# Sample index keys: gathers and their transposes issued apart, the transposes behind the products of the pair ahead

## The chip, the cores and the metric

The kernel runs on one core of a Trainium2 chip. The metric is the device time of one execution in microseconds; the figure given for a kernel is the median of several runs. A profiled execution gives the trace from which all rows below come.

## What is computed

The reference is one inference step of a decoder trunk of two layers (the constant in the reference, DEPTH = 2). A prompt of 1040 tokens (16 meta tokens and 1024 new ones) and a sample group of 8 sequences with 8 new tokens each share all weights. Each layer has three branches, a gated linear recurrence (HGRN2), a convolution module and a sparse attention, which are merged by gates and added to the residual stream. The change lies in the indexer of the sparse attention, which scores every key for every query; the 256 best keys are then attended to:

```python
def index_scores(qi, wi, ki):
    s = jnp.einsum('bqhd,bsd->bqhs', qi.astype(F32), ki.astype(F32))
    return jnp.einsum('bqhs,bqh->bqs', jax.nn.relu(s), wi.astype(F32) * IDX_SCALE)

def dsa_sample(...):
    ki_past = cache_kidx[page_table].reshape(nb, past, IDX_DIM)
    ki_all = jnp.concatenate([ki_past.astype(ki_new.dtype), ki_new], axis=1)
    sc = index_scores(qi, wi, ki_all)
    ...
```

For the sample group the index keys of the past (1024 keys of 64 numbers per sequence) lie in a paged cache and are fetched by the page table: eight sequences per layer, 256 KB each.

## The kernel before, in words

**The order of the work.** The kernel is written with a scheduling layer that gives every instruction its semaphores. TensorE runs in the order in which the program is written (the whole of it stands in a manual schedule for that engine), and so does VectorE from the start of a layer to the end of the mask stage. ScalarE, GpSimd and SyncE, which issues most transfers, are ordered by a planner from the program's order, its estimated durations and the times at which operands and buffers come free; once ordered, each of these queues is worked off strictly in turn.

**The filler.** A layer's dense projections are one stream of matmuls (L391, `stream`), cut into steps of three matmuls. Other stages call `fill(key)` to put so many steps between their own TensorE instructions, so that TensorE has work while they wait for other engines. A block of output needs 24 matmuls, 384 or 336 columns wide, into one of two `mm` tiles in PSUM; ScalarE evicts it (L204) to a tile `sp`. The weights of the stream come as 512 KB transfers on SyncE (L267), are rounded by ScalarE (`wh`, L269, the weight cast) and their remainder is formed on GpSimd (`wl`, L270, the weight split). In the same manner `taps(key)` puts steps of the depthwise convolution (L1503, L1504) into VectorE's order.

**The indexer.** It first prepares the prompt's keys, then scores six blocks of prompt queries with four heads each (the prompt's heads, `for i in range(7, 1, -1)`; behind each block GpSimd masks the diagonal, L814), and then comes to the sample. There the eight sequences are taken in four pairs, two groups of two pairs. For a sequence, GpSimd gathers 128 rows of eight keys by an indirect DMA (L887) into a tile `kir`, of which there are two. Four transposes on TensorE (L895) turn it into a PSUM tile `tp`, of which there are three. ScalarE copies its two halves (L899, L900) into the pair's tile `kib`, of which there is one. Two matmuls per sequence (L861, the products) multiply `kib` with the queries into the group's tile `lg`. So the next pair's copies cannot begin before this pair's products are done.

After two pairs the scores against the new keys follow (L865), then ScalarE's Relu, a matmul that adds up the heads (L835), and VectorE's additions into the score tile SC8 (L838 for the first group, L840 for the second and for the 16 meta queries, L876 and L877). Between transposes and products of a pair stand two `fill("ib")` of six steps each (36 matmuls) and two `taps("ts")`.

**Where the gathers and transposes stand.** `sample_kidx` issues the gather and the four transposes of one sequence and returns a function that makes the copies. It is called for pair 0 behind the prompt's heads and `fill("iw")`, and for pair i+1 right behind the copies of pair i: so the transposes of pair i+1 stand in TensorE's order ahead of the two `fill("ib")` and the products of pair i.

Of the kernel before, what the change touches and what calls it, by code (L numbers as in the profile page):

```python
# [154 lines left out]
def trunk(tc, a, o, depth=DEPTH):  # L155
# [35 lines left out]
    def lgt():  # L191
        return pair[0].tile([128, 1024], F32, name="lg", tag="lg")

    def tpt():
        return ptp.tile([128, 512], F32, name="tp", tag="tp")
# [7 lines left out]
    def act_(out, in_, fn, **kw):  # L203
        S.activation(out, in_, fn, **kw)  # L204
# [368 lines left out]
    def layer(l, hst, late):  # L573
# [46 lines left out]
        SC8 = scp.tile([128, NT], F32, name="SC8", tag="SC8")  # L620
        fill("ic")
        indexer(l, CTr, SC, SC8, fill, taps, act)
        ctr.close()
        tk1 = tks.enter_context(tc.tile_pool(name="tk1", bufs=1))
# [106 lines left out]
    def indexer(l, CTr, SC, SC8, fill, taps, act):  # L731
        with tc.tile_pool(name="ixc", bufs=1) as xc, tc.tile_pool(name="ixt", bufs=2) as xt:
# [28 lines left out]
            def qstack(t, rows):  # L761
                ps = tpt()
                for j in range(2):
                    T.transpose(ps[:, j * rows:(j + 1) * rows], CTr[0:rows, t, 256 + 128 * j:384 + 128 * j],
                                ident[0:rows, 0:rows])
                q = xt.tile([128, 2, 2, 128], F32R, name="qs", tag="qs")
                lo = ps[0:64, 0:2 * rows].rearrange("p (j n) -> p j n", j=2)
                hi = ps[64:128, 0:2 * rows].rearrange("p (j n) -> p j n", j=2)
                S.copy(q[0:64, :, 0, 0:rows], lo)
                S.copy(q[64:128, :, 1, 0:rows], hi)  # L770
                V.tensor_tensor(q[64:128, :, 0, 0:rows], lo, f(q[0:64, :, 0, 0:rows]), op=OP.subtract)
                V.tensor_tensor(q[0:64, :, 1, 0:rows], hi, f(q[64:128, :, 1, 0:rows]), op=OP.subtract)
                return q, lo, hi

            def qk(dst, q, h, rows, c0, c1):
                j, e = divmod(h, 2)
                T.matmul(dst, q[:, j, e, 0:rows], KIH[:, c0:c1], start=True, stop=False)
                T.matmul(dst, q[:, j, e, 0:rows], KIL[:, c0:c1], start=False, stop=True)
# [7 lines left out]
            for g in range(3):  # L786
# [4 lines left out]
                V.tensor_reduce(w1[0:m], w4[0:m], AX.X, OP.add)  # L791
                V.tensor_scalar(ws[0:m, g, :], cols[0:m, g, :], w1[0:m, 0:1], None, op0=OP.mult)
            fill("iq")
            for i in range(7, 1, -1):
                n = 128 * (i + 1)
                q = nxt[0]
                dst = SC[:, SCOFF[i]:SCOFF[i] + n]
                for h in range(4):
                    ps = lgt()
                    for c0 in range(0, n, 512):  # L800
                        c1 = min(n, c0 + 512)
                        qk(ps[:, c0:c1], q, h, 128, c0, c1)
                    if h == 1:
                        nxt = qstack(i - 1, 128) if i > 2 else qstack(8, 80)
                    fill("is", 7 - i)
                    rl = xt.tile([128, 1152], F32, name="rl", tag="rl")
                    act_(rl[:, 0:n], ps[:, 0:n], AF.Relu)
                    taps("ti", 7 - i)
                    if h == 0:
                        V.tensor_scalar(dst, rl[:, 0:n], wsc[:, i, 0:1], None, op0=OP.mult)  # L810
                    else:
                        V.scalar_tensor_tensor(dst, rl[:, 0:n], wsc[:, i, h:h + 1], dst, op0=OP.mult, op1=OP.add)  # L812
                dg = SC[:, SCOFF[i] + n - 128:SCOFF[i] + n]
                G.affine_select(dg, dg, pattern=[[-1, 128]], base=0, channel_multiplier=1, compare_op=OP.is_ge, fill=NEG)  # L814
# [10 lines left out]
            for h in range(4):  # L825
                j, e = divmod(h, 2)
# [4 lines left out]
            def gather(g, r):  # L831
                m = 128 if g < 2 else 64
                pg, pc = lgt(), pac.tile([128, 512], F32, name="ac", tag="ac")
                for (c0, c1), dst in zip(CH, (pg[0:80, 0:512], pg[0:80, 512:1024], pc[0:80, 0:80])):
                    T.matmul(dst, ws[0:m, g, :], r[0:m, c0:c1], start=True, stop=True)  # L835
                if g == 0:
                    S.copy(SC8[0:80, 0:1024], pg[0:80])
                    V.tensor_tensor(SC8[0:80, 1024:NT], pc[0:80, 0:80], cm80[0:80], op=OP.add)  # L838
                else:
                    V.tensor_tensor(SC8[0:80, 0:1024], SC8[0:80, 0:1024], pg[0:80], op=OP.add)  # L840
                    V.tensor_tensor(SC8[0:80, 1024:NT], SC8[0:80, 1024:NT], pc[0:80, 0:80], op=OP.add)

            fill("iw")

            kraw = [sample_kidx(l, e, xt) for e in range(2)]
            for g in range(2):
                ps = lgt()
                for b in (0, 2):
                    ki = xt.tile([128, 1024], F32, name="kib", tag="kib", bufs=1)
                    for e in range(2):  # L850
                        kraw[e](ki[64 * e:64 * e + 64])
                    taps("ts")
                    if 4 * g + b < 6:
                        kraw = [sample_kidx(l, 4 * g + b + 2 + e, xt) for e in range(2)]
                    fill("ib")
                    taps("ts")
                    fill("ib")
                    for n in range(2):
                        for e in range(2):
                            r, c0 = slice(64 * e, 64 * e + 64), 512 * (n ^ e)  # L860
                            T.matmul(ps[32 * (b + e):32 * (b + e) + 32, c0:c0 + 512],  # L861
                                     qs8[r, 4 * g + b + e].rearrange("p h q -> p (h q)"), ki[r, c0:c0 + 512],
                                     start=True, stop=True)
                px = tpt()
                T.matmul(px[:, 0:80], qs8[0:64, 4 * g:4 * g + 4].rearrange("p b h q -> p (b h q)"), ki8, start=True, stop=True)  # L865
                r = xt.tile([128, 1152], F32, name="rl", tag="rl")
                act_(r[:, 0:1024], ps, AF.Relu)
                act_(r[:, 1024:NT], px[:, 0:80], AF.Relu)
                fill("ir")
                gather(g, r)  # L870
                fill("ig")
# [6 lines left out]
            r = xt.tile([128, 1152], F32, name="rl", tag="rl")  # L878
# [5 lines left out]
    def gather_rows(dst, cache, l, bb):  # L884
        src = cache.rearrange("l n (g s) h d -> (l n g) (s h d)", s=8) if len(cache.shape) == 5 else \
            cache.rearrange("l n (g s) d -> (l n g) (s d)", s=8)
        G.indirect_dma_start(out=dst, out_offset=None, in_=src,  # L887
                             in_offset=bass.IndirectOffsetOnAxis(ap=rowid[:, l, bb:bb + 1], axis=0))

    def sample_kidx(l, bb, xt):  # L890
        raw = xt.tile([128, 8, 64], F32, name="kir", tag="kir")
        gather_rows(raw.rearrange("p s d -> p (s d)"), a["cache_kidx"], l, bb)
        ps = tpt()
        for j in range(4):
            T.transpose(ps[:, 128 * j:128 * j + 128], raw[:, 2 * j:2 * j + 2, :].rearrange("p j d -> p (j d)"), ident)  # L895

        def keys(ki):
            kv = ki.rearrange("p (n j e) -> p e j n", j=4, e=2)
            S.copy(kv[:, 0], ps[0:64].rearrange("p (j n) -> p j n", j=4))  # L899
            S.copy(kv[:, 1], ps[64:128].rearrange("p (j n) -> p j n", j=4))  # L900

        return keys
# [881 lines left out]
```

## Time and profile before

| | |
|---|---|
| median of 3 runs | 2891.84 us (2885.23 to 2892.67) |
| profiled execution, its own time | 2899.35 us |
| span of the profiled execution | 2897.4 us |
| instructions | 44994 |
| mean granted TensorE clock | 0.982 |

The profile counts for each engine the time in which an instruction of it ran. The timeline lists instructions in order of time; runs of equal instructions are merged (x8), and a bracket gives the time the engine had stood idle before and what ended it. PE is TensorE, DVE is VectorE, ACT is ScalarE, POOL is GpSimd. A granted clock of 1.00 is the full TensorE clock of 2.4 GHz, 0.50 is 1.2 GHz.

### The profile page before, as it was taken

To read this page: it belongs to the slowest core of one execution; us is meant where nothing else is said; L and a number is where in the kernel's file an instruction comes from. 1 tells how busy PE (TensorE), PEld (TensorE's weight loads), DVE (VectorE), ACT (ScalarE), POOL (GpSimd) and SP (SyncE) were. 2 spreads that over 40 slices of the span, in tenths; PEclk is the share of its full clock that TensorE was granted. 3 is DMA by queue.
4 is the path that set the end of the run, shared out by engine and by line. 5 is a ranking of instruction groups with operands and counts; after the bars stand their busy time and mean duration, and the time that the engine had idled before them with its cause. 6 is when DMAs were issued, how large, how long until landed. Compare 5 with 4: busy or idle time off the path is not lost. (4 is left out here: it accounts for less than half of the span.)

```text
span 2897.4 us, 44994 instructions
## 1 busy us (share of the span) xinstructions
PE 2751.2 (95%) x17094; PEld 2614.6 (90%) x17094; DVE 2120.3 (73%) x3832; ACT 1183.9 (41%) x2365; POOL 1249.3 (43%) x978
## 2 busy tenths in 40 slices
PE   7999899999998999989999998998999999999898
PEld 7999779999998898879999997898999989888798
DVE  5789887888969667445357798798899786774533
ACT  4324443332333556544341344422332345565432
POOL 3543344433434115756563342534444241158553
PEclk9999999999999999999999999999999999999999
DMA  4433233332244224656453233422331441256644
GB/s 153 152 93 101 91 122 124 115 124 94 98 157 152 76 68 154 213 190 190 149 170 95 88 102 101 166 77 103 119 130 62 158 151 57 87 162 219 198 156 150
DMA packets 192568, 374.14 MB, mean 129 GB/s; under 512 B 30656, under 2 KB 129696, under 8 KB 192288
## 3 DMA queue, kind: packets, MB, share of 16 engines
q1 hardware_dynamic: 166016, 272.21, 29.8%
q10 hardware_dynamic: 20448, 78.09, 6.7%
q0 software_dynamic: 5888, 20.97, 2.3%
q8 instruction: 134, 2.20, 0.3%
q14 instruction: 82, 0.67, 0.1%
HBM read 251.07 MB, written 122.40 MB: 129 GB/s over the span
## 5 line engine op out<-in xcount | busy, mean ns | idle before, releaser
L391 PE MATMUL mm<-xh,wh 128*128 128x384 f32 (+2 forms) x2656 | 887.9, 336 | 22.5 <-ACT sp L204 19.1
L391 PE MATMUL mm<-xl,wh 128*128 128x384 f32 (+2 forms) x2656 | 884.0, 335 | 0.0
L270 POOL TENSOR_TENSOR wl<-wr,wh 128x512 fp32r<-128x512 f32 x332 | 481.2, 1467 | 714.7 <-ACT wh L269 452.3
L391 PEld LDWEIGHTS mm<-xh,wh 128*128 128x128 f32 x2656 | 505.9, 190 | 36.8 <-ACT sp L204 24.5
L391 PE MATMUL mm<-xh,wl 128*128 128x384 f32 (+2 forms) x2656 | 530.4, 336 | 0.0
L391 PEld LDWEIGHTS mm<-xl,wh 128*128 128x128 f32 x2656 | 505.5, 190 | 7.1 <-issue 1.7
L391 PEld LDWEIGHTS mm<-xh,wl 128*128 128x128 f32 x2656 | 460.2, 191 | 6.2 <-issue 1.7
L923 DVE TENSOR_SCALAR_CACHE_REDUCE jk<-SC,F 80x1104 bf16<-80x1104 f32 (+6 forms) x448 | 448.8, 1002 | 8.4
L204 ACT ACTIVATE sp<-mm,vec 128x384 f32<-128x384 f32 (+1 forms) x356 | 198.6, 565 | 525.5 <-PE mm L391 509.9
L1503 DVE SCALAR_TENSOR_TENSOR cy<-up,vec,cy 128x1040 f32<-128x1040 f32 x240 | 333.1, 1388 | 0.4
L269 ACT CAST wh<-wr 128x512 fp32r<-128x512 f32 x352 | 203.5, 618 | 157.8 <-PE mm L391 76.6
L204 ACT ACTIVATE P<-P,nm 128x896 f32<-128x896 f32 (+7 forms) x128 | 99.5, 777 | 64.1 <-DVE nm L1028 62.2
L1044 DVE TENSOR_TENSOR pl<-tp,ph 128x512 fp32r<-128x512 f32 x144 | 97.7, 687 | 36.8 <-ACT ph L1043 36.1
L1504 DVE SCALAR_TENSOR_TENSOR cy<-us,vec,cy 128x64 f32<-128x64 f32 x240 | 118.3, 493 | 0.0
L1043 ACT CAST ph<-tp 128x512 fp32r<-128x512 f32 x144 | 83.2, 583 | 54.3 <-PE tp L1040 50.2
L1028 DVE CUSTOM_DVE_ANT_0 P<-sc,MB 128x512 f32<-128x512 f32 (+1 forms) x96 | 63.9, 667 | 56.5 <-PE sc L1022 55.7
L1353 PEld LDWEIGHTS lg<-hQ,hK 128*128 128x128 f32 x512 | 67.8, 210 | 28.0 <-issue 19.9
L1353 PE MATMUL lg<-hQ,hK 128*128 128x64 f32 x512 | 68.5, 292 | 25.5 <-DVE hQ L1382 25.4
L1032 DVE TENSOR_SCALAR P<-P,nm 128x896 f32<-128x896 f32 (+7 forms) x128 | 87.9, 687 | 4.3
L1040 PE MATMUL tp<-ident,P 128*128 128x128 f32 x576 | 87.5, 274 | 1.5 <-DVE P L1032 1.5
L204 ACT ACTIVATE rl<-lg 128x1024 f32<-128x1024 f32 (+6 forms) x54 | 42.6, 789 | 93.3 <-DVE SC L812 40.1
L287 PE MATMUL tp<-xh,wh 128*128 128x384 f32 (+2 forms) x240 | 79.0, 331 | 0.4 <-DVE z L1689 0.4
(454 smaller groups left out, 5914.7 us busy)
## 6 DMA issues: line engine op xcount, KB each, us to landing
wr<-in_wp SPq DMA_DIRECT2D x180, 512.0 KB
eg<-gateD SPq DMA_DIRECT2D x80, 184.0 KB
gateD<-sp ACTq DMA_DIRECT2D x24, 552.0 KB
gateD<-sp ACTq DMA_DIRECT2D x24, 544.0 KB
cr<-in_wc SPq DMA_DIRECT2D x16, 290.0 KB
gt<-gateD SPq DMA_DIRECT2D x24, 192.0 KB
za<-zaD SPq DMA_DIRECT2D x24, 192.0 KB
ggD<-sp ACTq DMA_DIRECT2D x8, 552.0 KB
```

Source lines behind the costliest of these rows:

```text
L204: S.activation(out, in_, fn, **kw)
L269: S.copy(wh[:, k:k + 4], wr[:, k:k + 4])
L270: (eng or G).tensor_tensor(wl[:, k:k + 4], wr[:, k:k + 4], f(wh[:, k:k + 4]), op=OP.subtract)
L391: T.matmul(ps, w, x, start=(j == 0), stop=(j == 23))
L923: V.tensor_scalar(jk[0:rows, 0:n], s, F.bitcast(F32)[0:rows, j:j + 1], None, op0=OP.is_ge, op1=OP.add, accum_out=cnt[0:rows, j:j + 1])
L1032: V.tensor_scalar(p[:, 0:n], p[:, 0:n], nm[:, 3:4], None, op0=OP.mult)
L1040: T.transpose(ps[:, 128 * c:128 * c + 128], P[c][:, 128 * kt:128 * kt + 128], ident)
L1043: S.copy(ph, ps)
L1044: V.tensor_tensor(pl, ps, f(ph), op=OP.subtract)
L1353: T.matmul(ps[:, 64 * c:64 * c + 64], K[:, 128 * c:128 * c + 128], up(Q[:, 128 * c:128 * c + 128], m), start=True, stop=True)
L1503: V.scalar_tensor_tensor(yp, up[:, j:j + 1040], w, yp, op0=OP.mult, op1=OP.add)
L1504: V.scalar_tensor_tensor(ys, us[:, :, j:j + 8], w, ys, op0=OP.mult, op1=OP.add)
```

## The change

`sample_kidx` is split in two: `kidx_rows` allocates `kir` and issues the gather; `kidx_turned` makes the four transposes and returns the copies. The gathers of pair 0 are issued ahead of the prompt's heads in the program's order, their transposes where they were. The gathers of pair i+1 stay where they were, right behind the copies of pair i; their transposes now come behind the products of pair i. Number and kind of all instructions, the buffers and the filler's steps are the same.

```diff
             fill("iq")
+
+            rows = [kidx_rows(l, e, xt) for e in range(2)]
             for i in range(7, 1, -1):
...
             fill("iw")
 
-            kraw = [sample_kidx(l, e, xt) for e in range(2)]
+            kraw = [kidx_turned(r) for r in rows]
             for g in range(2):
                 ps = lgt()
                 for b in (0, 2):
...
                     taps("ts")
                     if 4 * g + b < 6:
-                        kraw = [sample_kidx(l, 4 * g + b + 2 + e, xt) for e in range(2)]
+                        rows = [kidx_rows(l, 4 * g + b + 2 + e, xt) for e in range(2)]
                     fill("ib")
                     taps("ts")
                     fill("ib")
...
                                      start=True, stop=True)
+                    if 4 * g + b < 6:
+                        kraw = [kidx_turned(r) for r in rows]
                 px = tpt()
...
-    def sample_kidx(l, bb, xt):
+    def kidx_rows(l, bb, xt):
         raw = xt.tile([128, 8, 64], F32, name="kir", tag="kir")
         gather_rows(raw.rearrange("p s d -> p (s d)"), a["cache_kidx"], l, bb)
+        return raw
+
+    def kidx_turned(raw):
         ps = tpt()
         for j in range(4):
```

## Rows read from the trace of the kernel before

**Rows 1.** The page: busy us, share, instructions; and a group of evictions (mean ns).

```profile
PE 2751.2 (95%) x17094; PEld 2614.6 (90%) x17094; DVE 2120.3 (73%) x3832; ACT 1183.9 (41%) x2365; POOL 1249.3 (43%) x978
...
L204 ACT ACTIVATE sp<-mm,vec 128x384 f32<-128x384 f32 (+1 forms) x356 | 198.6, 565 | 525.5 <-PE mm L391 509.9
```

**Rows 2.** Waits of TensorE, whole run: us in total, times, longest.

```profile
PE tp L895 <- DMA kir<-in_cache_kidx,rowid: 7.8, 4, 3.4
...
PE tp L895 <- ACT kib L900: 4.6, 4, 1.7
...
PE lg L876 <- DVE SC L840: 1.4, 2, 0.8
```

**Rows 3.** Timeline of TensorE, layer 0, sample's pairs: start us, us, instruction, idle before.

```profile
316.99 1.03 PE L895 MATMUL tp<-ident,kir 128*128 128x128 f32 x8
...
321.27 0.63 PE L895 MATMUL tp<-ident,kir 128*128 128x128 f32 x4 [3.25 <-DMA kir<-in_cache_kidx,rowid]
322.75 0.63 PE L895 MATMUL tp<-ident,kir 128*128 128x128 f32 x4 [0.84 <-DMA kir<-in_cache_kidx,rowid]
...
330.96 1.91 PE L861 MATMUL lg<-kib,qs 64*32 64x512 f32 x8
...
335.16 0.65 PE L895 MATMUL tp<-ident,kir 128*128 128x128 f32 x4 [1.71 <-ACT kib L900]
...
350.66 0.66 PE L895 MATMUL tp<-ident,kir 128*128 128x128 f32 x4 [0.59 <-ACT kib L900]
...
357.52 1.91 PE L861 MATMUL lg<-kib,qs 64*32 64x512 f32 x8
```

**Rows 4.** The same timeline in layer 1.

```profile
1750.13 1.08 PE L895 MATMUL tp<-ident,kir 128*128 128x128 f32 x4 [3.42 <-DMA kir<-in_cache_kidx,rowid]
1751.51 1.08 PE L895 MATMUL tp<-ident,kir 128*128 128x128 f32 x4 [0.30 <-DMA kir<-in_cache_kidx,rowid]
...
1759.14 1.91 PE L861 MATMUL lg<-kib,qs 64*32 64x512 f32 x8
...
1763.33 0.66 PE L895 MATMUL tp<-ident,kir 128*128 128x128 f32 x4 [1.70 <-ACT kib L900]
```

**Rows 5.** Stretches: length; busy PE, PEld, DVE, ACT, POOL; granted clock, DMA, GB/s.

```profile
322.70:326.80 4.10, 4.05 (x17) 4.08 (x18) 4.10 (x6) 1.68 (x3) 3.34 (x3) 0.58 0.30 76
...
331.00:336.00 5.00, 3.29 (x19) 1.59 (x19) 5.00 (x9) 3.18 (x4) 1.13 (x1) 1.00 0.24 66
347.51:372.69 25.18, 24.59 (x135) 19.66 (x135) 25.18 (x33) 14.82 (x17) 4.27 (x3) 1.00 0.22 79
1775.69:1801.15 25.46, 24.88 (x136) 19.95 (x136) 25.46 (x34) 14.83 (x17) 4.62 (x3) 1.00 0.23 79
```

**Rows 6.** Pair 0's gathers, both layers: ns min/median/max, first and last start.

```profile
L887 POOL DMA_INDIRECT kir<-in_cache_kidx,rowid x2: 971/1252/1534, 184.6 to 189.5; - x2
...
L887 POOL DMA_INDIRECT kir<-in_cache_kidx,rowid x2: 996/1185/1374, 1614.3 to 1619.4; - x2
```

**Rows 7.** Timeline of GpSimd, layer 0: pair 1's second gather, two weight splits.

```profile
319.20 0.95 POOL L887 DMA_INDIRECT kir<-in_cache_kidx,rowid  x1 [0.30 <-issue]
...
325.94 2.75 POOL L270 TENSOR_TENSOR wl<-wr,wh 128x512 fp32r<-128x512 f32 x2 [0.23 <-issue]
```

**Rows 8.** Tile kir, layer 1's pairs 1 to 3: gather's time from issue to landing.

```profile
DMA to landing us min/median/max: 4.4/5.1/5.9
```

**Rows 9.** Timeline of ScalarE: copies in layer 0 and 1, and a cast.

```profile
332.91 1.09 ACT L899 COPY kib<-tp 64x512 f32<-64x512 f32 x1 [1.78 <-PE lg L861]
...
1791.40 1.20 ACT L900 COPY kib<-tp 64x512 f32<-64x512 f32 x1
1792.62 1.14 ACT L269 CAST wh<-wr 128x512 fp32r<-128x512 f32 x2
```

**Rows 10.** Waits of VectorE in the sample's stretch, layer 0 and layer 1.

```profile
DVE SC L838 <- PE ac L835: 9.1, 1, 9.1
...
DVE SC L838 <- PE ac L835: 8.6, 1, 8.6
```

## The prediction

> **What bounds the kernel now.** I read four views in this order. First the page's busy shares: TensorE works 95% of the span, VectorE 73%, ScalarE and GpSimd little over 40% [rows 1]. So time leaves this kernel where TensorE stands still or runs slow, and comes back wherever VectorE is late. Second, TensorE's waits over the whole run, for what the change can touch: the transposes L895 wait 7.8 us for the gathers of index keys and 4.6 us for the ScalarE copies that empty their PSUM tiles [rows 2]. Third, the timelines of the sample's stretch in both layers, to see where these waits lie: all between the end of the prompt's heads and the last pair's transposes. Fourth, VectorE's waits and busy time there, to see how far VectorE follows if TensorE comes earlier.
>
> In layer 0 the eight transposes of pair 0 end at 318.02. Those of pair 1 stand right behind them in TensorE's written order, and their gather is issued only then, because `kir` has two buffers that pair 0 held: TensorE idles 3.25 us, then 0.84 us for the second key block. After products 0, pair 2's second block waits 1.71 us for a PSUM tile, and pair 3's waits 0.59 us [rows 3]. Layer 1 repeats it with 3.42, 0.30 and 1.70 us, and what is left of the 4.6 us of copy waits, 0.6, at pair 3 [rows 2, 4]. The standing still has a second price. The granted clock is 0.58 of full in 322.7 to 326.8 and 1.00 in 331 to 336 behind it [rows 5]. Of the two levels (1.2 and 2.4 GHz) it is the lower one for most of that window, right after the 3.25 us idle.
>
> **The change part by part.** I add no instruction and take none away: 64 transposes, 16 gathers, 32 copies and 64 products stay. What changes is order, so the sum is one of waits.
>
> *The first gather ahead of the heads: 0.* The pair-0 gathers already start at 184.6 and 1614.3, over 100 us before their transposes, and TensorE's transposes 0 start without a wait for them [rows 3, 6]. Moved past: GpSimd's weight splits and six diagonal masks per layer; two issues of at most 1.5 us each stand ahead of them at worst, 3.0 us, and no row shows anyone waiting for them. I take 0; bounds -1 to +3.0 us per layer.
>
> *Transposes behind the products: pair 1's wait goes.* The new order on TensorE is transposes 0, twelve filler steps, products 0, transposes 1, twelve steps, products 1, and so on. Between the end of transposes 0 and transposes 1 now lie 36 filler matmuls and 1.91 us of products. 36 such matmuls take 6.2 us at full clock (351.32, the end of transposes 3, to 357.52) [rows 3], so the cover is 8.1 us. What it has to cover: the second gather of pair 1 starts on GpSimd at 319.20 and its block is used at 322.75, which is 4.7 us behind the end of transposes 0 [rows 3, 7]; margin 3.4 us. The longest landing of a `kir` gather is 5.9 us from issue [rows 8], which would still arrive 7.1 us behind it. So 3.25 + 0.84 us go in layer 0, 3.42 + 0.30 in layer 1. For pair 2 the new point is again 8.1 us behind transposes 1, but two weight splits (2.75 us together) may stand ahead of its gathers on GpSimd [rows 7]: 4.7 + 2.75 = 7.5, still inside. The half-clock stretch goes with the idle. What it costs in layer 0: the 36 matmuls between transposes 1 and products 0 took 323.38 to 330.96 = 7.6 us against about 6.1 for that mix: 1.5 us. In layer 1 the same takes 1752.59 to 1759.14 = 6.55, 0.45 too much, and the two groups of four transposes 1.08 instead of 0.63 us each: 0.9; together 1.35 us [rows 3, 4].
>
> *The PSUM waits go.* There are three `tp` tiles. Today transposes i+2 are written while the tiles of pair i+1 wait for products i, so a block finds none free. In the new order the copies of pair i are over before products i can start, and all three are free: 1.71 and 1.70 us go. The 0.6 us at pair 3 go from TensorE as well, but not from the time, see below.
>
> *What is newly late.* Copies i+1 used to start right at the end of products i (330.96 + 1.91 = 332.87, first copy at 332.91 [rows 3, 9]); now they wait for the first block's transposes too, 0.66 us more. Four copies at 1.09 to 1.20 us each take at most 4.8 us [rows 9], so they end 5.5 us behind products i, and products i+1 stand 1.3 (transposes) + 6.0 to 6.2 (steps) = 7.3 us behind. Margin 1.8 us: no wait. Behind the copies in ScalarE's queue stand the evictions of the filler, at most 0.6 us each by the mean of their group L204 on the page, 565 ns [rows 1]; the other `mm` buffer holds 24 matmuls (about 4.1 us), so they may cost up to 4.8 + 0.6 - 4.1 = 1.3 us per pair if each comes right at the start of the copies. Pair 1 of today has the same arrangement without a wait, so I take 0; bounds 0 to 1.3 us for six pairs.
>
> *VectorE's limit.* VectorE idles 9.1 us (layer 0) and 8.6 us (layer 1) before L838, the first score add, because it waits for TensorE [rows 10]. It can follow TensorE by that much. Behind L838 (347.51 and 1775.69) it is busy every moment of the 25.18 and 25.46 us to the next add L840 [rows 5], and TensorE then waits for that add, 1.4 us in both layers [rows 2]. So a gain behind L838 (pair 3's 0.6) is lost into that wait, and only the gains ahead of it count.
>
> *The sum.* Layer 0: 3.25 + 0.84 + 1.71 + 1.5 = 7.3 us; layer 1: 3.42 + 0.30 + 1.70 + 1.35 = 6.8 us. Both are under VectorE's 9.1 and 8.6 us, so both engines leave the stretch that much earlier, and all that follows takes its start from one of them. Total 14.1 us. Against the profiled execution (span 2897.4, its own time 2899.35 us) that is 2885.2; the median 2891.84 lies 7.5 us lower, so I predict 2891.84 - 14.1 = 2877.7 us. Most it could be: VectorE's whole slack, 9.1 + 8.6 = 17.7, gives 2874. Least without a new wait: 14.1 less 2 x 3.0 (first gather) less 6 x 1.3 (evictions) = 0.3, gives 2891.5.
>
> **A rule against it.** Products and transposes now follow each other without filler between. Today products 0, transposes and a 1.71 us idle lie together in 331 to 336 and the granted clock there is 1.00 [rows 3, 5]. The Trainium skill, "TensorE: Matmul & The Clock Gate", section "Part 4: PE-mode transpose", says that transposes don't count as busy time for the clock as matmuls do. By the row the denser order costs nothing; by the rule it could drop the clock, which is rival 2.
>
> **The rivals.**
> 1. *The gathers still don't land in time* (the change doesn't do what it says). GpSimd and its queue are ordered by the planner; if a split that waits for its weights stands ahead of a gather, transposes i+1 wait at their new place. For: two splits of 2.75 us do stand among the gathers on GpSimd [rows 7]. Against: 3.4 us of margin for pair 1. Price: pair 1's wait and clock loss return (4.09 + 1.5 and 3.72 + 1.35 = 10.7 us), the PSUM gain of 3.4 stays: 2888.4 us. Chance 0.11.
> 2. *The clock falls at the new bunches.* By the cost of one half-clock stretch, 1.5 us, at the six places where transposes follow products: 9 us of 14.1 given back, 2886.7 us. Against: the 1.00 in 331 to 336. Chance 0.07.
> 3. *Slower: ScalarE's queue holds the copies.* If the planner places the two weight casts (1.14 us) ahead of a pair's copies and their weights have not landed, the copies wait behind them. It decides once the hold is over the 1.8 us margin; then products stand still. Price: a hold like the gather's 3.4 us + 1.14 us less 1.8 = 2.7 us, and 1.5 us of clock, 4.2 us; three cast pairs in each layer's stretch give 25 us: 2877.7 + 25 = 2903 us. For: ScalarE takes its work in order, and the casts do lie in this stretch. Against: today the casts stand behind the four copies, as at 1792.62 [rows 9]. Chance 0.12.
>
> **How the numbers follow.** Forecast 0.70, rivals 0.11, 0.07 and 0.12. 0.3% of the median is 8.7 us, about what a measurement of this kernel can tell from no change: under 2883.1 is faster, over 2900.5 slower. The forecast's own range is 2871 to 2884 (14.1 with the spread of the runs, 6.6 us below the median). Faster: 0.63 of the forecast's 0.70, and 0.04 of rivals 1 and 2: 0.67. Slower: rival 3 nearly whole, 0.11. The same: 0.22. The range runs from 2868 (all of VectorE's slack, and the lowest run's 6.6 us under the median) to 2891, about the least gain without a new wait; it takes in rivals 1 and 2 and leaves out rival 3.
>
> **What would show it.** Right: transposes of pairs 1 to 3 without a wait for a gather or a copy; granted clock 1.00 through both stretches; L838 starting about 7 us earlier than 347.51; VectorE's idle ahead of L838 down to about 1.8 us in both layers; the wait at L876 no smaller. Wrong: a wait of products L861 for the copies, evictions moved behind copies with the filler waiting, a half-clock window elsewhere, or the 7 us found again as a wait for VectorE or a load between the sample's stretch and the end of the layer.

## The result and the profile after

The changed kernel takes 2877.78 us (median of 5 runs, 2872.07 to 2882.85) beside 2892.67 us for the kernel before on the same chip: 14.9 us less, ratio 0.9946 with a 95% interval of 0.993 to 0.9963. Two further sets of runs on other occasions gave 0.9943 (0.9926 to 0.996) and 0.995 (0.9938 to 0.9961). Predicted were 2877.7 us and 14.1 us less.

TensorE's waits in the profiled execution after, whole run (us in total, times, longest). Line numbers shift with the lines that an edit adds, so the same instruction has another number in each kernel:

```profile
PE mm L391 <- ACT sp L204: 18.8, 13, 4.5
...
PE lg L880 <- DVE SC L842: 5.0, 2, 2.5
```

The transposes, now L902, are not in the list at all: the 7.8 us of waits for gathers and the 4.6 us for copies of [rows 2] are gone. What has grown is the wait for VectorE's second score add (L840 before, L842 now), from 1.4 to 5.0 us.

The timeline of TensorE after, in layer 0, answers to [rows 3]:

```profile
321.35 1.03 PE L902 MATMUL tp<-ident,kir 128*128 128x128 f32 x8
...
328.42 1.91 PE L863 MATMUL lg<-kib,qs 64*32 64x512 f32 x8
330.26 1.09 PE L902 MATMUL tp<-ident,kir 128*128 128x128 f32 x8
...
337.28 1.91 PE L863 MATMUL lg<-kib,qs 64*32 64x512 f32 x8
339.12 1.09 PE L902 MATMUL tp<-ident,kir 128*128 128x128 f32 x8
...
371.56 0.45 PE L880 MATMUL lg<-KIH,qt 128*64 128x512 f32 x1 [2.49 <-DVE SC L842]
```

No bracket stands at products or transposes. Products 0 start 7.07 us behind the start of transposes 0; before it was 330.96 - 316.99 = 13.97. Stretches of the profile after, with the columns of [rows 5]: from transposes 0 to the first score add, and from there to the second, in layer 0 and then in layer 1.

```profile
321.30:344.00 22.70, 22.70 (x132) 17.92 (x131) 21.43 (x28) 16.82 (x21) 12.23 (x9) 1.00 0.39 125
344.07:370.30 26.23, 25.00 (x137) 20.03 (x136) 26.23 (x33) 12.57 (x15) 4.76 (x4) 1.00 0.28 92
1733.80:1756.50 22.70, 22.70 (x132) 17.92 (x131) 21.44 (x28) 16.79 (x21) 12.21 (x9) 1.00 0.40 126
1756.58:1782.80 26.22, 25.01 (x137) 20.04 (x136) 26.21 (x33) 12.61 (x15) 4.74 (x4) 1.00 0.28 92
```

In the first part of both layers TensorE is busy every moment, at a granted clock of 1.00. In the second part VectorE is busy every moment, as before, but the part has grown: 26.2 us against 25.18 and 25.46 [rows 5].

Where did the time come from? The first instruction of the stretch lies 4.4 us later in the trace after (321.35 against 316.99), and ahead of it the trace after has 17.1 us at half clock, the one before 3.4. This goes with the execution and not with the change: the trace of experiment 4, which issues the first gathers early as well, has 3.4 us there and starts these transposes at 315.91. So I count from the start of transposes 0 within each trace. VectorE's adds after and, behind "...", the last add of layer 0:

```profile
344.07 0.24 DVE L840 TENSOR_TENSOR SC<-ac,cb 80x80 f32<-80x80 f32 x1 [1.34 <-PE ac L837]
344.23 2.78 DVE L1510 SCALAR_TENSOR_TENSOR cy<-up,vec,cy 128x1040 f32<-128x1040 f32 x1
...
370.30 1.20 DVE L842 TENSOR_TENSOR SC<-SC,lg 80x1024 f32<-80x1024 f32 x1
...
376.36 1.22 DVE L842 TENSOR_TENSOR SC<-SC,lg 80x1024 f32<-80x1024 f32 x1 [4.71 <-PE lg L837]
```

| us from the start of transposes 0 | before, layer 0 / 1 | after, layer 0 / 1 | gain |
|---|---|---|---|
| first score add starts | 30.53 / 30.01 | 22.72 / 22.72 | 7.8 + 7.3 = 15.1 |
| second score add starts | 55.71 / 55.46 | 48.96 / 48.96 | 6.75 + 6.5 = 13.25 |
| last score add ends | 62.98 / 62.73 | 56.23 / 56.24 | 13.2 |

The span of the profiled execution fell by more, 22.1 us (2897.4 to 2875.3). That is not the change alone: outside these stretches the trace after has 11 us less of half clock than the one before, worth at most 5.6 us by my estimate (half of the time at half clock). The medians are the measure for the whole; the stretches say where it comes from.

### The profile page after: what moved, and what is told of

It reads as the page before. It is cut to its first block, busy times and chain, and to the rows that moved or that the text cites. A ratio compares the mean times of both kernels' runs of the same rounds, so it can differ in the third digit from the quotient of the medians.

```text
span 2875.3 us, 44996 instructions
## 1 busy us (share of the span) xinstructions
PE 2739.9 (95%) x17094; PEld 2606.9 (91%) x17094; DVE 2118.8 (74%) x3832; ACT 1183.6 (41%) x2365; POOL 1250.8 (44%) x978
## 5 line engine op out<-in xcount | busy, mean ns | idle before, releaser
L391 PE MATMUL mm<-xh,wh 128*128 128x384 f32 (+2 forms) x2656 | 886.1, 336 | 22.2 <-ACT sp L204 18.8
L1039 DVE TENSOR_SCALAR P<-P,nm 128x896 f32<-128x896 f32 (+7 forms) x128 | 87.9, 687 | 4.3
```

Of the source, the lines that this page charges most:

```text
L391: T.matmul(ps, w, x, start=(j == 0), stop=(j == 23))
L1039: V.tensor_scalar(p[:, 0:n], p[:, 0:n], nm[:, 3:4], None, op0=OP.mult)
```

## The experiments

My theory was the prediction's: the whole gain comes from where the transposes stand, it consists of three parts (a gather issued too late, the half clock behind the idle, a PSUM wait), the earlier first gather is worth nothing, and behind the first score add VectorE sets the pace. The rivals stand in the expectations. Ratios are to the kernel before, run beside.

**1. Only the transposes moved.**

```diff
-            rows = [kidx_rows(l, e, xt) for e in range(2)]
             for i in range(7, 1, -1):
...
+            rows = [kidx_rows(l, e, xt) for e in range(2)]
             kraw = [kidx_turned(r) for r in rows]
```

> The changed kernel, but with the gathers of pair 0 issued at their old place, behind the prompt's heads and the filler in the program's order. My theory (the whole gain comes from where the transposes stand): the same as the changed kernel, about 15 us under the kernel before, ratio 0.994 to 0.996; pair 0's gathers still start over 100 us ahead of their transposes. Rival (the earlier place of the first gather carries part of the gain, by itself or through the planner's order): at least 4 us slower than the changed kernel, ratio 0.997 or more.

Measured: 0.9952 (0.9934 to 0.9971), the same as the changed kernel. Products 0 start at 7.07, the first add at 22.73, the second at 48.97 us behind transposes 0, as after. The gathers of pair 0 start at 186.6 and 191.1 us, over 125 us ahead of their transposes, without being written there.

**2. Only the first gather moved.**

```diff
-                        rows = [kidx_rows(l, 4 * g + b + 2 + e, xt) for e in range(2)]
+                        kraw = [kidx_turned(kidx_rows(l, 4 * g + b + 2 + e, xt)) for e in range(2)]
...
-                    if 4 * g + b < 6:
-                        kraw = [kidx_turned(r) for r in rows]
```

> Only the other half: pair 0's gathers ahead of the heads, and the transposes of pair i+1 right behind their gathers, ahead of the filler and the products of pair i, as in the kernel before. My theory: no change, ratio 0.998 to 1.002, with waits of the transposes for gathers of about 4 us a layer and for copies of 2.3 us a layer. Rival (first gather matters): faster by 4 us or more.

Measured: 1.0012 (0.9997 to 1.0027). TensorE's waits in that run:

```profile
PE tp L900 <- DMA kir<-in_cache_kidx,rowid: 8.1, 4, 3.4
PE tp L900 <- ACT kib L905: 4.5, 4, 1.7
```

They are nearly those of [rows 2]. So the two halves of the change are told apart: the first gather gives nothing, the transposes everything that could be measured.

**3. The old order, but buffers for pair 1's gathers.**

```diff
     def sample_kidx(l, bb, xt):
-        raw = xt.tile([128, 8, 64], F32, name="kir", tag="kir")
+        if bb in (2, 3):
+            raw = xt.tile([128, 1152], F32, name="rl", tag="rl")[:, 0:512].rearrange("p (s d) -> p s d", s=8)
+        else:
+            raw = xt.tile([128, 8, 64], F32, name="kir", tag="kir")
```

> The kernel before, with its order, but the gathers of pair 1 (sequences 2 and 3) go to the two free buffers of another tile instead of the two buffers that pair 0 holds, so they can be issued before pair 0's transposes. My theory (the loss was a gather issued too late plus the half clock behind the idle; the PSUM tiles are a third, smaller part): transposes of pair 1 no longer wait for a gather, granted clock 1.00 in the stretch, but the second block now waits about 1.7 us for a PSUM tile, as pair 2's does; stretch up to the first score add about 4 us shorter in each layer, in all 6 to 9 us under the kernel before, ratio 0.997 to 0.998. Rival (the place of the transposes behind the products is what counts, the gather's time is hidden or replaced by the PSUM wait): within 3 us of the kernel before.

Measured: 0.9966 (0.9953 to 0.998), 2884.57 against 2894.56 us. Its timeline of TensorE in layer 0:

```profile
318.77 1.03 PE L898 MATMUL tp<-ident,kir 128*128 128x128 f32 x8
319.64 0.60 PE L898 MATMUL tp<-ident,rl 128*128 128x128 f32 x4
321.65 0.66 PE L898 MATMUL tp<-ident,rl 128*128 128x128 f32 x4 [1.40 <-ACT kib L903]
328.35 1.91 PE L861 MATMUL lg<-kib,qs 64*32 64x512 f32 x8
...
332.56 0.66 PE L898 MATMUL tp<-ident,kir 128*128 128x128 f32 x4 [1.71 <-ACT kib L903]
```

With the rows there in time, the gather's wait and the half clock go without any new order (granted clock 1.00 in 318.8 to 342), and a wait for one of the three PSUM tiles comes in at pair 1, as at pair 2. The first add starts 26.12 us behind transposes 0 in layer 0 and 26.14 in layer 1: 4.4 and 3.9 us earlier than before, where the changed kernel has 7.8 and 7.3. So up to the first add a buffer buys a little over half, and the order buys the rest by keeping both the gathers and the PSUM tiles out of the way. In the whole time this difference does not show: beside 10.0 us here stand 12.9 in experiment 1 and 12.3 in experiment 4, run on the same chip, and the intervals overlap.

**4. The gathers written late.**

```diff
-                    if 4 * g + b < 6:
-                        rows = [kidx_rows(l, 4 * g + b + 2 + e, xt) for e in range(2)]
                     fill("ib")
...
                     if 4 * g + b < 6:
+                        rows = [kidx_rows(l, 4 * g + b + 2 + e, xt) for e in range(2)]
                         kraw = [kidx_turned(r) for r in rows]
```

> The changed kernel with the gathers of pairs 1 to 3 issued only behind the products, together with their transposes; pair 0's stay ahead of the heads. My theory (issuing apart is what hides the gather): the transposes wait at each of the three pairs. The gather was usable 4.7 us behind the end of the transposes before it in the kernel before, and its buffers are free long before, but by the program's order the planner may still issue it early, since nothing but the buffers holds it: then nothing changes and the time is that of the changed kernel, ratio 0.994 to 0.996. Rival (the program's place of the gather decides): three waits of 3 to 5 us a layer and 1.5 us of clock each, 24 us or more in all, slower than the kernel before by 5 to 15 us.

Measured: 0.9952 (0.9936 to 0.9969), like the changed kernel. No transposes waited. So the first half of my expectation, a wait at each pair, was wrong, and its second half held. GpSimd's timeline and the next transposes on TensorE:

```profile
316.79 1.06 POOL L890 DMA_INDIRECT kir<-in_cache_kidx,rowid  x1 [4.79 <-PE tp L901]
318.15 0.95 POOL L890 DMA_INDIRECT kir<-in_cache_kidx,rowid  x1 [0.30 <-issue]
```

```profile
315.91 1.03 PE L901 MATMUL tp<-ident,kir 128*128 128x128 f32 x8
324.83 1.09 PE L901 MATMUL tp<-ident,kir 128*128 128x128 f32 x8
```

The gathers go out 0.9 us behind the start of the transposes that free their buffers, though the program names them 8 us later. On GpSimd, which the planner orders, the buffer's release set the start here, not the place in the program; on TensorE, whose order is written, the place does. So it is not the early place of the gather in the program that hides it, but the late place of the transposes.

**5. The changed kernel again, and convolution steps behind the last add.**

```diff
-                    taps("ts")
+                    if 4 * g + b < 6:
+                        taps("ts")
                     fill("ib")
...
                 fill("ig")
+                if g:
+                    taps("ts")
```

> The changed kernel itself, as the measure for the two others on the same chip: ratio to the kernel before 0.993 to 0.9965; from pair 0's transposes to the end of VectorE's second score add 56.2 us in both layers, TensorE waiting 2.5 us a layer at L880 for VectorE.

> The changed kernel, with one group of convolution steps (four steps of about 1.4 us on VectorE) taken from the last pair of the sample and put behind the second group's score add, where VectorE idles 4.7 us. My theory (behind the first score add VectorE is what bounds the stretch now, and 0.8 to 1.1 us a layer of TensorE's gain was lost there, besides the gain at pair 3): the wait at L880 goes, the stretch ends at 53 to 54.5 us instead of 56.2 in both layers, and the time is 3 to 5 us under the changed kernel. Rival (the convolution as a whole is due at the same moment, so moving a part of it moves only the wait): the stretch ends at 56 us or the convolution's norm behind it waits as much longer, and the time is that of the changed kernel within 2 us.

Measured: the changed kernel 0.9943, 2881.47 us; with the steps moved 0.9965 (0.995 to 0.9979), 2888.14 us: 6.7 us slower by the medians, though the two intervals overlap a little. The stretch did end at 53.7 us in both layers and the wait at L880 went, as my theory said. But the convolution ended later, 52.56 instead of 49.03 us behind transposes 0, and its norm waits for that. TensorE's wait behind the stretch in layer 0 (us, times, longest), the changed kernel and then this one:

```profile
PE tp L1531 <- POOL nsq L1528: 0.8, 2, 0.5
```

```profile
PE tp L1534 <- POOL nsq L1531: 5.6, 1, 5.6
```

And 380 to 420 us (columns of [rows 5]), again first the changed kernel:

```profile
380.00:420.00 40.00, 33.95 (x177) 30.70 (x176) 35.59 (x62) 20.09 (x37) 25.08 (x21) 0.96 0.31 109
```

```profile
380.00:420.00 40.00, 30.61 (x140) 27.91 (x141) 30.89 (x50) 17.61 (x33) 20.46 (x17) 0.83 0.23 79
```

The 2.5 us came back as 4.8 us of wait in layer 0 (3.7 in layer 1), and the granted clock from 380 to 420 us was 0.83 instead of 0.96. The rival had the mechanism, that the wait only moves, but not the time: it expected no more than 2 us of difference. It looks as if the end of the convolution were what bounds; experiment 7 tests this by moving steps the other way.

**6. Filler into the new wait.**

```diff
                 fill("ig")
+                fill(5 * g)
```

> The changed kernel, with five more filler steps (15 matmuls, about 2.5 us) on TensorE ahead of L880, where it now stands 2.5 us waiting for VectorE. My theory (TensorE is bound by its work from there on, and the wait is a hole that work of later stages can fill): the wait falls under 0.5 us, the stretch still ends at 56.2 us, and the filler is missing later in no place that needs it: 2 to 5 us under the changed kernel. Rival (the later stage that loses five steps of filler waits as long): the same as the changed kernel within 1.5 us.

Measured: 1.0182 (1.0163 to 1.0202), 2948.29 us, 67 us slower than the changed kernel. Neither expectation held. The wait at L880 was filled as meant, but TensorE's waits for `hQ`, a tile of the recurrence that VectorE forms, rose from 24.3 to 59.4 us, and the time at half clock in the whole trace from 87.9 to 161.2 us. ScalarE's timeline at one of the recurrence's heads in layer 0, the changed kernel and then this one:

```profile
633.35 1.14 ACT L269 CAST wh<-wr 128x512 fp32r<-128x512 f32 x2 [0.89 <-issue]
634.40 1.12 ACT L204 ACTIVATE hK<-hG 128x1104 f32<-128x1104 f32 x1
```

```profile
656.04 0.58 ACT L204 ACTIVATE sp<-mm,vec 128x384 f32<-128x384 f32 x1 [3.62 <-PE mm L391]
656.52 1.11 ACT L204 ACTIVATE sz<-az 128x1104 f32<-128x1104 f32 x1
657.54 1.11 ACT L204 ACTIVATE hK<-hG 128x1104 f32<-128x1104 f32 x1
```

The load of `hG`, from which `hQ` is formed, is issued at about the same time in both (628.9 and 632.1 us), and in this run it lands 5.7 us after its issue. But its sigmoid (`hK<-hG`) starts 23 us later, behind five evictions of the filler in ScalarE's queue, most of which wait for TensorE. With five steps shifted per layer the order of that queue is another. Why was not tested: the planner's choice and the filler's own shift, which also moves all later blocks of output, were not told apart.

**7. Convolution steps earlier, in the changed kernel and in the one before.**

```diff
-        "tr": (2400, 2400, 2400, 2400, 2400, 2400, 2400, 600, 0)
+        "tr": (2400, 2400, 2400, 2400, 2400, 2400, 2400, 600, 4200)
```

> The changed kernel, with 4200 units more of convolution steps (three steps, about 4.2 us on VectorE) behind the rotation of the last row tile of the indexer's projection, where VectorE idles 5.9 us in layer 0 and 17.5 us in layer 1 ahead of L752; as many fewer are then left at the end of the sample's stretch. My theory (the end of the convolution on VectorE bounds the changed kernel's stretch, and moving steps behind it only moves the wait, as the run with steps behind the last add showed): the convolution ends about 4 us earlier, the wait at L880 falls from 2.5 us to nothing, the stretch ends at 53.5 to 54 us instead of 56.2, and the convolution's norm does not wait longer; 3 to 6 us under the changed kernel, if the planner's order of the later queues stays. Rival (any shift of steps unsettles the planner's order, as five filler steps did): no faster than the changed kernel, with new waits of hQ or of evictions further on.

> The kernel before, with the same three convolution steps moved ahead. My theory: there VectorE waits 9.1 and 8.6 us for TensorE ahead of the first score add, so an earlier convolution only lengthens that wait; what remains is the wait of TensorE at L876, 0.6 and 0.8 us, and the end of the convolution. Stretch end 62 to 63 us as before, time within 3 us of the kernel before, ratio 0.998 to 1.002. Rival (VectorE's work there always counts): 4 us or more faster, as in the changed kernel.

Measured: in the changed kernel 0.9939 (0.9923 to 0.9955), 2875.81 us; in the kernel before 1.0006 (0.9995 to 1.0017). In the first the stretch ends at 53.53 us in both layers. VectorE's wait in 200 to 215 us, the changed kernel and then this one:

```profile
DVE ki L752 <- ACT KIL L750: 5.9, 1, 5.9
```

```profile
DVE ki L752 <- ACT KIL L750: 1.5, 1, 1.5
```

The steps go into idle time of VectorE, and the convolution ends 44.3 us behind transposes 0 instead of 49.0. TensorE's wait at L880 is gone; VectorE now waits 1.3 us for TensorE ahead of the second add. So the pace there is TensorE's again.

In the kernel before, the moved steps bring nothing, but not in the way I expected. VectorE's waits in layer 0 of that run:

```profile
DVE SC L838 <- PE ac L835: 9.3, 1, 9.3
DVE SC L840 <- PE lg L835: 9.1, 2, 5.4
```

The wait ahead of the first add has hardly grown in layer 0 (9.1 before). The freed time stands ahead of the second add, where VectorE was busy before and now waits 3.8 us, and ahead of the last one, 5.4 instead of 4.7. The stretch still ends at 62.9 us: there TensorE sets the end. As the first comparison did not separate this kernel from the changed one, both ran again side by side:

> The changed kernel once more, side by side with the run below: ratio to the kernel before 0.993 to 0.9965.

> The changed kernel with three convolution steps moved ahead, again, now beside the changed kernel on the same chip. My theory (2.7 us a layer saved in the stretch's end stay): ratio to the kernel before 0.0015 to 0.002 lower than that of the changed kernel beside it, 4 to 6 us. Rival (given back behind the stretch): the two ratios within 0.0007 of each other, 2 us.

Measured: the changed kernel 0.995 (0.9938 to 0.9961), 2881.71 us; with the steps earlier 0.9933 (0.9921 to 0.9945), 2875.97 us. The median is 5.7 us lower both times (the first time on two chips, the second on one), but the ratio by 0.0004 the first time and by 0.0017, 5 us, the second; the stretch is at least 2.7 us shorter in each layer. The intervals overlap, so this version is clearly better than the kernel before, likely better than the changed one, and the last is not settled.

## Why the prediction was right

**First gather: 0.** Shown by experiments 1 and 2.

**Gather wait and half clock.** Right in mechanism and size: no bracket at the transposes, clock 1.00 up to the second add, and experiment 3 takes these two away alone and gains 4.4 and 3.9 us up to the first add, the price of its own PSUM wait already paid. By the terms of the sum it should have gained 5.6 and 5.1 less that wait of 1.4, so 4.2 and 3.7. No run takes the half clock away without the gather's wait, so the 1.5 and 1.35 us for the clock are not shown by themselves.

**PSUM waits.** They went, as said. The gain up to the first add was 7.8 and 7.3 us, 0.5 more in each layer than my 7.3 and 6.8. I had left a small term out: two groups of four transposes with a gap take 0.66 us each [rows 3], eight in a row 1.09 us together; that is 0.2 us per pair, 0.5 for the two pairs ahead of the first add.

**What is newly late: 0.** Right: the copies of pair 1 end at 335.76 in layer 0, 1.5 us ahead of products 1 (I said 1.8), and TensorE's wait for evictions in the whole run is 18.8 us, 19.1 before.

**VectorE's limit.** Right, and this is the term that was mis-sized. VectorE's idle ahead of the first add fell to 1.34 us (I said 1.8), and the gain at pair 3 was lost, as said. But VectorE's work behind the add took 26.2 instead of 25.18 and 25.46 us, so 1.1 and 0.8 us more were lost. The convolution step right behind the first add shows it: 2.78 us in both layers beside 1.29 for its neighbours. Before, it took 1.69 and 1.99 us, and the differences, 1.09 and 0.79, are the whole of it. VectorE before, layers 0 and 1, and after, layer 1 (layer 0 stands above):

```profile
347.67 1.69 DVE L1503 SCALAR_TENSOR_TENSOR cy<-up,vec,cy 128x1040 f32<-128x1040 f32 x1
1775.85 1.99 DVE L1503 SCALAR_TENSOR_TENSOR cy<-up,vec,cy 128x1040 f32<-128x1040 f32 x1
...
1756.75 2.78 DVE L1510 SCALAR_TENSOR_TENSOR cy<-up,vec,cy 128x1040 f32<-128x1040 f32 x1
```

GpSimd beside it, before in layers 0 and 1, and after in layer 0:

```profile
345.76 2.50 POOL L270 TENSOR_TENSOR wl<-wr,wh 128x512 fp32r<-128x512 f32 x2 [8.10 <-ACT wh L269]
1774.22 2.51 POOL L270 TENSOR_TENSOR wl<-wr,wh 128x512 fp32r<-128x512 f32 x2 [7.92 <-ACT wh L269]
...
343.36 2.54 POOL L270 TENSOR_TENSOR wl<-wr,wh 128x512 fp32r<-128x512 f32 x2
```

A weight split runs there each time, and the step is longer by nearly as much as the split still runs beside it: 0.40, 0.70 and 1.49 us longer than 1.29, beside 0.59, 0.88 and 1.67 us of split. With the first add earlier, more of the split falls on the step. The Trainium skill ("SBUF — State Buffer", "Who interferes with whom") says that a VectorE instruction with two inputs in SBUF contends with a GpSimd instruction that reads SBUF; both are such, and the trace agrees with 2.78 against 1.29 us. The same holds where split and step meet otherwise: 1.70 us in experiment 3, with 0.60 us of split beside the step, and 2.08 us in experiment 7, with 0.97. The wait of TensorE for the second add is 2.5 us a layer, where I said only "no smaller".

**Sum.** 14.1 us were forecast, the stretches of the profiled execution gave 13.2, the medians 14.9 and, in the two further sets, 13.9 and 14.7. That it came so close is in part luck: the 1.0 us that I had left out and the 1.9 us that VectorE took have opposite signs. And in 4 of the 10 stretches in the traces of the changed kernel and of experiments 1 and 4, the 2.5 us wait at L880 has a half-clock stretch right behind it (granted clock 0.52 from 369.8 to 373.2 in one of them), and the last add ends at 57.7 us instead of 56.2. This is the half-clock window elsewhere that I had named as a sign of being wrong. With it the stretches give 10 to 13 us. Where the other few us of the medians come from is open.

**Rivals.** Late gathers: none in any run of the new order. Lower clock at products and transposes side by side: the granted clock was 1.00 there, though eight transposes now follow the products of pairs 0 to 2 directly. So the trace does not show what the Trainium skill ("TensorE: Matmul & The Clock Gate", "Part 4: PE-mode transpose") says of transposes, that they don't count as busy time like matmuls; with 1.09 us of transposes in a row it cost nothing here. ScalarE's queue: in layer 0 the casts came behind pair 0's copies (327.20) and among pair 2's (341.22), and no products waited. Experiment 6 shows such harm from the order of ScalarE's queue, at another place and with another edit.

## What to carry to other kernels

An instruction that waits for a transfer holds all that is written behind it on its engine; move the consumer behind work that is ready, and check that the buffer the transfer needs is free that much earlier. Before counting a gain on one engine, read how long the next engine idles at the meeting point: here 9.1 and 8.6 us, and the gain stopped where that other engine was busy throughout. Work moved behind a stage's end came back here as the next stage's wait; work moved into idle time ahead of it did not, though what that gained in the whole time is not settled.

## What I had not expected

Five filler steps moved ahead in each layer cost 67 us, and the first cause that the trace shows is the order of ScalarE's queue over 200 us further on. And the half-clock stretches differ from one execution to another: the profiled spans of the changed kernel were 2875.3, 2882.4 and 2876.7 us, with 87.0, 87.9 and 85.1 us at half clock, against 105.0 in the profile before.
